# Six changes against the last waits of TensorE: row fetch, fifth output buffer, zero products, earlier first loads, halved last tile and a branch without SyncE stores in a 4096 matrix product with GELU

## The chip, the cores and the metric

The kernel runs on one core of a Trainium2 chip. The metric is the device time of one launch in microseconds, the median of the fast runs. A profiled run also has a span, from the first to the last instruction; it is about 1.6 us shorter than the run's time.

## The reference

```python
m, k, n = 4096, 4096, 4096            # a, b: float32, normal random numbers
x = np.matmul(a, b)
return 0.5 * x * (1 + np.tanh(np.sqrt(2 / np.pi) * (x + 0.044715 * x**3)))
```

## The kernel before

The product is done in float16 by a seven-product (Strassen-like) scheme over the four quadrants of `a` and `b`, in 16 output blocks (`gi`, 0 to 15). Each product (`s`, 0 to 6) has four steps (`q`) of 16 matmuls of 512 columns. VectorE forms the sums of quadrant pieces, TensorE multiplies and accumulates in two chains of banks of PSUM, its result memory (X and Y), ScalarE copies PSUM out and applies GELU, SyncE stores, and GpSimd loads with a cast to float16. An A piece is loaded into one of two staging buffers and then transposed by VectorE.

```python
PRODUCTS = [("Y", "11", ("12", "22", 1)),              # chain, A operand, B operand
            ("X", ("11", "12", -1), "22"),
            ("X", ("12", "22", -1), ("21", "22", 1)),  # third product: needs A22 and B21
            ("X", ("11", "22", -1), ("11", "22", -1)), # fourth product
            ... ]
```

For the first block the data are not there yet. Its first half of the inner dimension is done by 16 plain steps (numbers 0 to 15) as pieces arrive, and only the second half by the seven products (steps 16 on, two for each product).

A numerical check of the inputs ends in a flag. Its six statistics go through DRAM to become one row; if the flag is 0, a slow general path runs in a branch at the end.

```python
    def verdict(d):                     # called in the last block, at product 2
        for f in (0, 3):
            ...
            nc.sync.dma_start(out=row[f], in_=d...)      # fetch: behind the stores in SyncE's queue
        v = ...                          # 24 small VectorE instructions on the row
    def new_y():
        return pool.tile([P, NC], F32, name="y", tag="y", bufs=4)
    for n, step in enumerate(steps):
        for fn, args in before.get(n, ()): fn(*args)
        make_sums(...)                   # VectorE, two steps ahead of TensorE
        flush()                          # finish waiting output tiles: addition, GELU, store
        combine()
        plain(n) or multiply(*step)
with tc.If(stands == 0):
    general_path(tc, a, b, out)          # its stores: SyncE
```

## Time and profile before

| | |
|---|---|
| median | 1592.03 us at first, 1592.19 over all runs of the comparison |
| span of the profiled run | 1589.5 us |
| TensorE busy | 1570.7 us, 99% |
| lost to waits in the first 140 us, with the half clock after one of them | 9.2 us |
| lost at the verdict, with the half clock after it | 5.3 us |
| after the last product | 7.1 us |

Busy time of 99% leaves little, so the timeline of TensorE has to be read against its own grid: a group of 32 products takes 6.906 us from start to start, and each group that starts later than that has lost the difference. Half clock means a stretch in which the trace's clock records grant TensorE half of its clock. A DMA lands when the last of its sixteen shares is reported (those of the kernel's last store between 1586.06 and 1586.97). The lines are shown in the prediction.

### The profile page before, as it was taken

How to read it: one execution, taken by the hardware profiler on the slowest of the kernel's cores; microseconds unless marked ns; L12 is line 12 of the kernel's file. 1: busy time of each engine (PE TensorE's matmuls, PEld its weight loads, DVE VectorE, ACT ScalarE, POOL GpSimd, SP SyncE). 2: the span in 40 equal slices, each digit the busy share in tenths (PEclk: the TensorE clock that was granted, in tenths of full speed). 3: DMA queues.
4: the chain of work that ended last, by engine and by line, in shares of the span. 5: the costliest groups of instructions: out<-in, count | busy, mean ns of one | idle time of the engine just before them, and what ended most of it. 6: DMA issues, size and time to landing. Idle time of an engine off the chain costs nothing. (4 is left out here: it accounts for less than half of the span.)

```text
span 1589.5 us, 19678 instructions
## 1 busy us (share of the span) xinstructions
PE 1570.7 (99%) x7244; PEld 710.1 (45%) x7244; DVE 1229.0 (77%) x1370; ACT 520.9 (33%) x714; POOL 539.1 (34%) x980
## 2 busy tenths in 40 slices
PE   9999999999999999999999999999999999999998
PEld 3444444444444444444444444444444444444443
DVE  1498888967887888895878778887687778988675
ACT  0026454311122545531111344551212145454111
POOL 7663442430334144341124423245021443414300
PEclk9999999999999999999999999999999999999999
DMA  9998793891957488586597937679387886837702
GB/s 173 188 225 176 111 187 70 153 176 38 200 99 153 93 132 159 107 172 120 95 159 111 187 73 147 130 132 180 60 137 128 133 159 107 170 81 136 151 21 81
DMA packets 225048, 211.14 MB, mean 133 GB/s; under 512 B 20144, under 2 KB 192176, under 8 KB 224944
## 3 DMA queue, kind: packets, MB, share of 16 engines
q0 software_dynamic: 187648, 142.67, 61.1%
q1 hardware_dynamic: 37296, 67.13, 11.7%
q8 instruction: 59, 0.97, 0.2%
q14 instruction: 45, 0.37, 0.1%
HBM read 285.22 MB, written 67.11 MB: 222 GB/s over the span
## 5 line engine op out<-in xcount | busy, mean ns | idle before, releaser
L303 PEld LDWEIGHTS <-aS 128*128 128x128 f16 x4960 | 485.8, 98 | 590.7 <-issue 4.2
L173 POOL DMA_DIRECT2D bR<-in_b_dram x832 | 448.9, 544 | 705.5 <-DVE bS L276 335.1
L276 DVE TENSOR_TENSOR aS<-aT 128x2048 f16<-128x2048 f16 x310 | 376.5, 1221 | 154.0 <-PE accX L303 120.4
L303 PE MATMUL accX<-bS,aS 128*128 128x512 f16 x1984 | 432.8, 380 | 3.9 <-DVE bS L276 3.4
L276 DVE TENSOR_TENSOR bS<-bR 128x2048 f16<-128x2048 f16 x310 | 376.8, 1220 | 72.8 <-PE accX L303 62.1
L303 PEld LDWEIGHTS <-aT 128*128 128x128 f16 x1984 | 194.2, 98 | 236.0 <-issue 2.1
L391 ACT ACTIVATE y<-y 128x512 f32<-128x512 f32 x192 | 118.8, 631 | 338.9 <-DVE y L400 338.9
L303 PE MATMUL accY<-bS,aT 128*128 128x512 f16 x992 | 216.9, 379 | 1.8 <-DVE bS L276 1.8
L303 PE MATMUL accX<-bS,aT 128*128 128x512 f16 x992 | 216.7, 379 | 0.0
L303 PE MATMUL accY<-bS,aS 128*128 128x512 f16 x992 | 216.7, 379 | 0.0
L303 PE MATMUL accX<-bR,aS 128*128 128x512 f16 x992 | 216.7, 379 | 0.0
L303 PE MATMUL accY<-bR,aS 128*128 128x512 f16 x992 | 216.7, 379 | 0.0
L146 POOL DMA_DIRECT2D stage<-in_a_dram x144 | 90.0, 631 | 247.4 <-DVE aT L159 180.4
L400 DVE TENSOR_TENSOR energy<-energy,square 128x1024 bf16<-128x1024 bf16 x240 | 165.0, 688 | 9.2 <-ACT square L197 5.4
L197 ACT ACTIVATE square<-aT 128x1024 bf16<-128x1024 f16 x120 | 123.5, 1052 | 70.7 <-DVE energy L400 70.4
L364 ACT COPY x<-accX 128x512 f32<-128x512 f32 x128 | 74.8, 587 | 218.2 <-PE accX L303 218.2
L197 ACT ACTIVATE square<-bR 128x1024 bf16<-128x1024 f16 x120 | 123.1, 1052 | 62.4 <-DVE energy L400 62.3
L159 DVE STREAM_TRANSPOSE aT<-stage 128x2048 uint32<-128x2048 uint32 (+1 forms) x36 | 74.2, 2068 | 43.7 <-DMA stage<-in_a_dram 43.6
L364 ACT COPY m<-accX 128x512 f32<-128x512 f32 x64 | 37.2, 581 | 214.9 <-PE accX L303 214.2
L391 ACT ACTIVATE y<-accX 128x512 f32<-128x512 f32 x64 | 38.3, 598 | 101.4 <-PE accX L303 101.4
L400 DVE TENSOR_TENSOR x<-accX,x 128x512 f32<-128x512 f32 x64 | 43.9, 691 | 22.6 <-ACT y L391 21.6
L400 DVE TENSOR_TENSOR y<-accY,m 128x512 f32<-128x512 f32 x64 | 42.6, 688 | 13.5 <-ACT m L364 13.3
(37 smaller groups left out, 338.9 us busy)
## 6 DMA issues: line engine op xcount, KB each, us to landing
bR<-in_b_dram POOLq DMA_DIRECT2D x832, 128.0 KB, 5.3
out_dram<-y SPq DMA_DIRECT2D x256, 256.0 KB, 6.0
stage<-in_a_dram POOLq DMA_DIRECT2D x112, 256.0 KB, 6.9
stage<-in_a_dram POOLq DMA_DIRECT2D x32, 128.0 KB, 5.0
row<-seen_d SPq DMA_DIRECT2D x2, 1.5 KB, 2.2
seen_d<-seen SPq DMA_DIRECT2D x1, 3.0 KB, 7.5
```

The costliest lines, as they stand in the source:

```text
L146: nc.gpsimd.dma_start(out=s[g * Q : (g + 1) * Q, x : x + n, :], in_=a_v[kh * CH + c, g, :, x0 : x0 + n, :],)
L159: nc.vector.transpose(dst[:, :, x, :], src[:, :, x, :])
L173: nc.gpsimd.dma_start(out=t[g * Q : (g + 1) * Q, e::2, :], in_=b_v[kh * CH + c, g, e, :, :, n0 : n0 + NC],)
L197: nc.scalar.activation(t[:, :], src, ACT.Square)
L276: nc.vector.tensor_tensor(out=t[:, :], in0=part(tiles, blk, o[0], q), in1=part(tiles, blk, o[1], q), op=ALU.add if o[2] > 0 else ALU.subtract,
L303: nc.tensor.matmul(acc[:, :], sa[:, j // 2, i * P : (i + 1) * P, j % 2], sb[:, j, :], start=start and j == 0, stop=stop and j == 3, skip_g ...
L364: nc.scalar.copy(out=t[:, :], in_=src[:, :])
L391: nc.scalar.activation(y[:, :], src[:, :], ACT.Gelu_apprx_tanh)
L400: nc.vector.tensor_tensor(out=o[:, :], in0=x[:, :], in1=y[:, :], op=op)
```

## The change

The intent is to remove the remaining waits of TensorE and to shorten both ends. It has six parts: the row is fetched right after the statistics are written; a fifth output buffer; ten products with zero weights fill a known wait, so that the array's clock is not lowered (it was 0.5 for 3.41 us after that wait of 2.62 us); one transpose is moved a step earlier and the first A piece is loaded whole; the last tile is finished by column halves; the general path stores through GpSimd, so that the branch has no SyncE stores to wait for (SyncE's stores report on eight semaphores, called lanes here).

```diff
-    def verdict(d):
-        row = {}                                   # fetch of the row: moved to the end of gather()
+        return row
+    def verdict(row):
@@ halves of the last tile (products() takes a column slice n)
+    def last(gi, i, sa, sb):
+        y, m1 = new_y(), post.pop(("x7", i))
+        for h in range(2):
+            n = slice(h * NC // 2, (h + 1) * NC // 2)
+            products(banks["Y", i], sa, sb, i, False, True, n)
+            if h == 0:
+                flush()
+            nc.vector.tensor_tensor(out=y[:, n], in0=banks["Y", i][:, n], in1=m1[:, n], op=ALU.add)
+            emit(gi, i, 1, 1, y, y, n)
@@ fifth buffer
-        return pool.tile([P, NC], F32, name="y", tag="y", bufs=4)
+        return pool.tile([P, NC], F32, name="y", tag="y", bufs=5)
@@ zero products
+    def idle(n):
+        for _ in range(n):
+            nc.tensor.matmul(banks["X", 0][:, :], post["none"][:, :], b_tiles[0, "12", 0][:, 0, :],
+                             start=False, stop=False, skip_group_check=True)
+    before[4].append((idle, (N_IDLE,)))            # N_IDLE = 10
@@ order of the first loads
-        (8, "T21_0 B12_1 B22_1 A11_1"),
+        (7, "T21_0"),
+        (8, "B12_1 B22_1 A11_1"),
-            for h in (0, 1) if what[4] == "0" else (None,):
+            for h in (0, 1) if what[4] == "0" and what != "A11_0" else (None,):
@@ general path
-                nc.sync.dma_start(out=out[t * P : (t + 1) * P, bass.ds(n0, NC)], in_=y[:, :])
+                nc.gpsimd.dma_start(out=out[t * P : (t + 1) * P, bass.ds(n0, NC)], in_=y[:, :])
... (cuts: signatures and the zeroed weights)
```

## The prediction

Passages of the text below that no trace or run of this case shows are cut, and the cuts are marked. The forecast came to 4.42 + 2.30 + 2.17 + 1.35 - 0.1 + 0.85 = 11.0 us. One term has lost its ground: the -0.1 of the halves is their gain of 0.06 less an allowance of 0.2 us at the last store, and that allowance is cut. Without it the sum would be 11.2 us.

> **What bounds the kernel now.** I read the page's first line, then the waits of TensorE, then its timeline, then the two places where that timeline has holes, and last the records after the final matmul. The page and TensorE's list of waits:
>
> ```profile
> span 1589.5 us, 19678 instructions
> ...
> PE 1570.7 (99%) x7244; PEld 710.1 (45%) x7244; DVE 1229.0 (77%) x1370; ACT 520.9 (33%) x714; POOL 539.1 (34%) x980
> ```
>
> ```profile
> PE accX L303 <- DVE bS L276: 3.4, 1, 3.4
> PE accY L332 <- DMA bR<-in_b_dram: 2.6, 1, 2.6
> PE accY L332 <- DVE aT L159: 2.0, 1, 2.0
> PE accY L303 <- DVE bS L276: 1.8, 1, 1.8
> PE accX L315 <- DVE table L531: 1.3, 1, 1.3
> PE accX L303 <- DVE aS L276: 0.5, 1, 0.5
> ```
>
> TensorE is the bound: 7200 real products that the change does not touch. Everything to be won lies in six waits, in what follows them, and in the ends of the span. The timeline of TensorE alone tells more than the waits:
>
> ```profile
> 13.72 7.07 PE L332 MATMUL accY<-bR,aT 128*128 128x512 f16 x32
> 20.62 7.07 PE L332 MATMUL accX<-bR,aT 128*128 128x512 f16 x32
> 30.31 8.75 PE L332 MATMUL accY<-bR,aT 128*128 128x512 f16 x32 [2.62 <-DMA bR<-in_b_dram]
> 38.90 7.07 PE L332 MATMUL accX<-bR,aT 128*128 128x512 f16 x32
> 47.98 27.80 PE L332 MATMUL accY<-bR,aT 128*128 128x512 f16 x128 [2.01 <-DVE aT L159]
> ...
> 97.00 7.07 PE L303 MATMUL accX<-bS,aS 128*128 128x512 f16 x32 [0.51 <-DVE aS L276]
> ...
> 133.47 7.07 PE L303 MATMUL accY<-bS,aT 128*128 128x512 f16 x32 [1.77 <-DVE bS L276]
> ```
>
> Thirty-two products take 6.906 us from start to start (13.72 to 20.62), 0.2158 us each. Against that grid the stretch from 20.62 should have handed over at 27.53 and did so at 30.31: 2.78 us lost. The stretch from 30.31 took 8.59 us to the next start instead of 6.91: another 1.68 us, because the products ran at half speed. The wait at 47.98 cost 2.17 us and no clock. Those at 97.00 and 133.47 cost 0.66 and 1.93. After that there is no hole until the verdict, near the end:
>
> ```profile
> 1507.89 7.07 PE L303 MATMUL accX<-bS,aS 128*128 128x512 f16 x32
> ...
> 1510.73 1.22 SPq L234 DMA_DIRECT2D row<-seen_d  x2
> ...
> 1512.91 0.31 DVE L240 TENSOR_REDUCE v<-row 1x1 f32<-1x128 f32 x1 [2.44 <-DMA row<-seen_d]
> 1513.52 1.23 DVE L240 TENSOR_REDUCE v<-row 1x1 f32<-1x128 f32 x5 [0.30 <-DMA row<-seen_d]
> ...
> 1518.39 11.78 PE L303 MATMUL accX<-bS,aS 128*128 128x512 f16 x46 [3.43 <-DVE bS L276]
> ```
>
> VectorE stands 2.74 us (2.44 + 0.30) before the verdict's reductions, because SyncE fetched the row only after the last stores ahead of it in its queue; the sums that TensorE needs come behind them. TensorE should have gone on at 1514.80 and did at 1518.39 (3.59 lost). The 96 products to the next group boundary, at 1540.79, took 22.40 us instead of 20.72: 1.68 us of half clock again.
>
> [...] the clock fell after waits of 2.6 and 3.4 us and held after 2.0, 1.8 and 0.5. [...] the row fetch, moved next to the write of the scratch, will hold SyncE's queue for that write's 7.5 us (the page's table of DMA issues). [...] the stores at the end land 2.0 us after issue at the least and 3.6 at most here.
>
> **The change part by part.**
>
> Row fetch ahead. The scratch is written at 1484.40 and lands at 1491.9; the two row fetches follow (0.6 us of issue, 2.2 us to land each), so the row is there near 1495, 15 us before VectorE wants it. The one store held behind them (issued at 1484.83 now) starts near 1493; with the next output tile written near 1507 nobody wants its buffer. VectorE's 2.74 us of waiting go. Its sums end 2.74 us earlier, and TensorE's loss goes from 3.59 to 0.85 us: the 24 small verdict instructions (about 3 us) still stand before the sums. 0.85 us is under every wait that left the clock alone, so the 1.68 goes too. Gain 2.74 + 1.68 = 4.42 us.
>
> Ten zero products. They sit before the step that starts at 30.31. At 0.216 us they take 2.16 us from 27.53, to 29.69. The B piece waited for landed at 30.17. The first A piece in four DMAs of 256 KB instead of eight of 128 KB costs GpSimd some 2.5 us instead of 4.7 (0.64 against 0.58 us an issue), and in the first nine microseconds the DMA engines moved 100 to 185 GB/s against some 200 later, which is worth 1 to 1.9 us of earlier landing; so I take the piece to be there by 29.69. The step then starts at 29.69 (0.62 earlier) at full clock (1.68). Gain 2.30 us; if the landing does not move, 1.8. The first real product stays at 13.72: the 44 warm-up products end there.
>
> Transpose one step earlier. At 43.49 VectorE runs four additions (to 46.77) that no product waits for, then the transpose that TensorE waits for. The pieces for its two halves landed at 40.70 and 43.42. Moved ahead of the additions, the halves end near 41.9 and 44.7; TensorE, by now 2.3 us early, wants them at 43.5 and 47.0. No wait is left. Gain 2.17 us.
>
> Fifth output buffer. At 127.45 VectorE waits 3.18 us for the store of an earlier tile; the four tiles follow four landings (127.33, 128.74, 130.06, 131.47), and the sum that TensorE wants starts behind the last at 132.20. With five buffers the first tile finds a free one and the rest wait for the first three landings: the last ends near 130.87 and the sum starts 1.33 us earlier. Gain 1.35 of the 1.93.
>
> Last tile by halves. The last products end at 1582.4 either way. ScalarE's activation of the tile before ends at 1582.98; two half activations follow. From 512 columns at 0.587 us and 1024 at 1.052 a half is about 0.40, so ScalarE ends at 1583.78 instead of 1583.84. It has become the bound and the halves gain 0.06. The last store lands at 1586.97, its slowest sixteenth 0.6 us behind the others: [...] Net loss 0.1.
>
> Branch without store lanes. After the last landing (1586.97) SyncE passes five more lane waits (to 1587.33), then twelve waits of a second list (to 1588.12), 0.07 us each. The instruction order of the changed kernel shows the first list gone and SyncE waiting in the second, where the last store's lane is followed by only four or five. 1.2 us become about 0.35. Gain 0.85.
>
> Sum: 4.42 + 2.30 + 2.17 + 1.35 - 0.1 + 0.85 = 11.0 us. 1592.03 - 11.0 = 1581.0.
>
> **The rivals.** First, a gain at the start that is given back: from 60 to 100 us VectorE and the DMA queue are the tight chain. If the second A piece still lands at 65.45, VectorE's work from there (transposes 2.31, sums 1.2 each, the additions) reaches the four copies before the step at 97.00 only 3.8 us earlier while TensorE wants 4.47: some 0.7 us come back as a longer wait there. For it: the DMA engines are 90% busy or more to 60 us. Against it: VectorE waits for TensorE 3.7 + 0.4 us in that stretch, so it can follow. This makes 1581.7. Second, the verdict may get no cheaper if the row is late or another wait holds VectorE: the page's 7.5 us says it is not; otherwise 1585.4. Third, the zero products might be too few: if the clock falls all the same or the B piece comes later, 1583. Fourth, a gain that no wait shows, such as stores that overtake loads: I see none; TensorE's floor of 7200 x 0.2158 = 1553.8 us, plus 13.72 at the start and 7.1 at the end, is a span of 1574.6, only 4 us below the 1578.5 of my sum.
>
> **Range and chances.** The parts are independent and each is uncertain by half a microsecond to one. I take 1578.9 to 1584.3. Two per cent would be 32 us, three times all that is there to be won, so faster by that much is all but excluded; slower would need a new wait of 43 us.
>
> **What would show it.** TensorE's waits should be a list with no entry above 1.5 us; the step now at 30.31 should start near 29.7 with 32 products in 7.07 us; no wait for the transpose; the wait at 97.00 still there, 0.5 to 1.3 us, some 4.4 us earlier on the clock; the one at 133.47 about 0.6; the verdict's about 0.85, with no half-speed weight loads after it; VectorE's wait for the row gone. From the last store's landing to the end of the span there should be some 1.6 us, not 2.5. I would be wrong if a halved clock shows up after a wait under 2 us, or if the early stretch gives back more than a microsecond.

## More of the kernel before

The quadrant pieces are called by quadrant and half of the inner dimension: B21/1 is the second half of B's lower left quadrant.

The loads are issued from GpSimd's queue, in this order (in the trace of the kernel before A22/1 waits 6.21 us for its staging buffer and goes out at 68.18, and B21/1 follows it at 70.72):

```python
for n, whats in (                       # step number: A/B load a piece, T transposes an A piece
    (0, "A11_0 B12_0 T11_0 B11_0 A12_0 B22_0 B21_0 A21_0"),
    (4, "T12_0 A22_0"),
    (8, "T21_0 B12_1 B22_1 A11_1"),
    (10, "T22_0 A12_1"),
    (14, "T11_1 A22_1 B21_1 B11_1"),    # A22_1 waits for a staging buffer that T11_1 frees
    ...
```

Runs of one kernel spread by 2 us and more, and the 95% intervals of the ratios are about 0.13% (2 us) to either side. Parts worth less than that are therefore judged from stretches of the traces, not from medians.

## The result, and the profile after

The changed kernel takes 1583.76 us (median of 6, 1583.09 to 1585.01) against 1592.19 us for the kernel before in the same rounds (6 runs, 1591.26 to 1593.13). The ratio is 0.9948, interval 0.9935 to 0.9961. Ratios here are the mean time of one kernel's fast runs over that of the other's of the same rounds, so not quite the ratio of the medians. The gain of 8.4 us lies inside the predicted range, but it is 2.6 us short of the predicted 11.0.

The waits of TensorE in the changed kernel (total, times, longest, in us):

```profile
PE accX L304 <- DVE aS L277: 1.8, 1, 1.8
PE accX L304 <- ACT m L390: 1.6, 1, 1.6
PE accX L304 <- DVE bS L277: 1.5, 2, 0.9
PE accX L319 <- DVE zeros L311: 1.4, 1, 1.4
PE accY L304 <- DVE y L385: 0.7, 1, 0.7
```

The 2.6, 2.0 and 3.4 us of before are gone, but 1.8, 1.6, 0.9 and 0.7 us stand there that did not exist. TensorE's timeline tells where:

```profile
13.62 7.07 PE L344 MATMUL accY<-bR,aT 128*128 128x512 f16 x32
...
27.43 2.32 PE L326 MATMUL accX<-bR,none 128*128 128x512 f16 x10
29.59 7.07 PE L344 MATMUL accY<-bR,aT 128*128 128x512 f16 x32
...
43.41 27.79 PE L344 MATMUL accY<-bR,aT 128*128 128x512 f16 x128
...
86.02 1.90 PE L304 MATMUL accX<-bS,aS 128*128 128x512 f16 x8 [0.93 <-DVE bS L277]
89.56 5.34 PE L304 MATMUL accX<-bS,aS 128*128 128x512 f16 x24 [1.64 <-ACT m L390]
96.69 7.07 PE L304 MATMUL accX<-bS,aS 128*128 128x512 f16 x32 [1.79 <-DVE aS L277]
```

The start goes as planned. The zero products run at 27.43, the next step starts at 29.59 at full clock, and the step that stood at 47.98 starts at 43.41: 4.57 us ahead. The first block's fourth product, at 97.00 before, starts at 96.69. Of the lead 0.31 us is left; three waits in a row, at 86.02, 89.56 and 96.69, took the rest. VectorE's timeline has the reason:

```profile
80.68 1.23 DVE L277 TENSOR_TENSOR aS<-aT 128x2048 f16<-128x2048 f16 x1
84.74 1.23 DVE L277 TENSOR_TENSOR bS<-bR 128x2048 f16<-128x2048 f16 x1 [2.83 <-DMA bR<-in_b_dram]
85.88 1.22 DVE L277 TENSOR_TENSOR aS<-aT 128x2048 f16<-128x2048 f16 x1
...
88.15 2.68 DVE L426 TENSOR_TENSOR y<-accY,m 128x512 f32<-128x512 f32 x4
```

The sum for the third product waits 2.83 us for a B load. The load's records say that it is B21/1, whose last DMA landed at 84.20. In the kernel before the same piece landed at 82.40, and the same sum started at 84.52, since VectorE was busy with other work until then:

```profile
83.38 1.23 DVE L276 TENSOR_TENSOR aS<-aT 128x2048 f16<-128x2048 f16 x1
84.52 1.22 DVE L276 TENSOR_TENSOR bS<-bR 128x2048 f16<-128x2048 f16 x1
```

The load was in time by 2.1 us, unseen.

The verdict goes as predicted:

```profile
1489.00 1.22 SPq L231 DMA_DIRECT2D row<-seen_d  x2
...
1505.65 7.07 PE L304 MATMUL accX<-bS,aS 128*128 128x512 f16 x32
...
1508.14 1.48 DVE L241 TENSOR_REDUCE v<-row 1x1 f32<-1x128 f32 x6
...
1513.25 17.00 PE L304 MATMUL accX<-bS,aS 128*128 128x512 f16 x78 [0.53 <-DVE bS L277]
```

The row's fetch goes out at 1489.00, when the write of the scratch (1482.16) has landed, 6.8 us after its issue, where 7.5 were written; SyncE waited 6.5 us for it. So the row is asked for 19 us before its use, the six reductions run without a wait, and TensorE loses 0.69 us (1512.56 on the grid, 1513.25 in fact) with no half clock after it: the next group, 96 products on, starts at 1533.97, 20.72 us later.

The end, first before and then after (VectorE's addition and ScalarE's activation of the last tile; TensorE's last four products):

```profile
1582.49 0.69 DVE L400 TENSOR_TENSOR y<-accY,x 128x512 f32<-128x512 f32 x1 [0.17 <-PEq L552]
1583.21 0.63 ACT L391 ACTIVATE y<-y 128x512 f32<-128x512 f32 x1 [0.23 <-DVE y L400]
```

```profile
1575.41 0.41 DVE L385 TENSOR_TENSOR y<-accY,x 128x256 f32<-128x256 f32 x1
...
1575.88 0.60 PE L304 MATMUL accY<-bS,aS 128*128 128x256 f16 x4 [0.73 <-DVE y L385]
...
1576.51 0.42 DVE L385 TENSOR_TENSOR y<-accY,x 128x256 f32<-128x256 f32 x1 [0.69 <-PE accY L304]
1576.97 0.42 ACT L417 ACTIVATE y<-y 128x256 f32<-128x256 f32 x1 [0.51 <-DVE y L385]
```

TensorE's second half now waits 0.73 us until VectorE has read the first half. Both lie in the same PSUM tile, which is the likely reason; a version with two tiles was not run. So the work that should overlap runs in turn.

The two profiled runs differ by 7.57 us of span. It can be split at the starts of product groups, and the last landing (the fourth product itself takes 6.91 us in both and is left out):

| stretch | before, us | after, us | won |
|---|---|---|---|
| start to the first block's fourth product | 97.00 | 96.69 | 0.31 |
| first block's fifth product to second block's second (fifth buffer) | 36.46 | 34.53 | 1.93 |
| from there to the last block's second product | 1353.70 | 1353.70 | 0.00 |
| from there to its fifth product (verdict) | 46.71 | 42.13 | 4.58 |
| from there to the last store's landing (halves) | 46.17 | 46.76 | -0.59 |
| last landing to the end (branch) | 2.50 | 1.18 | 1.32 |

### The profile page after: what moved, and what is told of

The parts are those of the page before. It is cut to its first block, busy times and chain, and to the rows that moved or that the text cites. A ratio compares the mean times of both kernels' runs of the same rounds, so it can differ in the third digit from the quotient of the medians.

```text
span 1581.9 us, 19694 instructions
## 1 busy us (share of the span) xinstructions
PE 1569.4 (99%) x7258; PEld 710.7 (45%) x7258; DVE 1228.2 (78%) x1372; ACT 520.0 (33%) x715; POOL 535.5 (34%) x976
## 4 chain that ended last, share of the span: by engine, by line
PE 93%; DMA 2%; POOL 2%; DVE 1%; issue 1%; ACT 0%; DVEq 0%; ACTq 0%; POOLq 0%
PE accX L304 53%; PE accY L304 40%; DMA stage<-in_a_dram 2%; POOL stage L147 1%; POOL bR L174 1%; DMA bR<-in_b_dram 1%; DVE bS L277 0%; DVE y L426 0%; DVE aS L277 0%; DVE aT L160 0%; DVE v L241 0%; ACT m L390 0%; ACT y L417 0%; DVE y L385 0%; DVE ok L251 0%
## 5 line engine op out<-in xcount | busy, mean ns | idle before, releaser
L417 ACT ACTIVATE y<-y 128x512 f32<-128x512 f32 (+1 forms) x193 | 118.7, 627 | 337.5 <-DVE y L426 336.6
L304 PE MATMUL accY<-bS,aS 128*128 128x512 f16 (+1 forms) x996 | 216.9, 378 | 0.7 <-DVE y L385 0.7
```

Source lines behind the costliest of these rows:

```text
L304: nc.tensor.matmul(acc[:, n], sa[:, j // 2, i * P : (i + 1) * P, j % 2], sb[:, j, n], start=start and j == 0, stop=stop and j == 3, skip_g ...
L417: nc.scalar.activation(y[:, n], src[:, n], ACT.Gelu_apprx_tanh)
```

## The experiments

The theory that the trace suggests: the lead of 4.5 us at the start is real, but it runs into the arrival of B21/1, so the early parts win next to nothing (feed theory). The rival is that of the prediction: each part keeps its gain, and what is missing was lost elsewhere (additive theory). Twelve kernels were run in three sets; each set was timed beside the kernel before on its own chip.

**1. Early parts undone.** The four other parts stay.

```diff
-    before[4].append((idle, (N_IDLE,)))
-        (7, "T21_0"),
-        (8, "B12_1 B22_1 A11_1"),
+        (8, "T21_0 B12_1 B22_1 A11_1"),
-            for h in (0, 1) if what[4] == "0" and what != "A11_0" else (None,):
+            for h in (0, 1) if what[4] == "0" else (None,):
```

> The changed kernel with its three early parts undone (no zero products, the transpose back in its old step, the first A piece in eight DMAs); fifth buffer, row fetch, halves and branch stay. Feed theory (the lead won before 72 us is eaten up to the step near 97 us by VectorE's wait for the second half of B's lower left piece, which the DMA queue brings no earlier than before): slower than the changed kernel by only 0.3 us (0 to 1), TensorE's step there starts at 97.0 as before. Additive theory (my prediction): slower by 4.5 us, since each early part keeps its own gain.

Measured: 1584.61 us, ratio to before 0.9947 (0.9933 to 0.9962), where the changed kernel has 0.9948. The three early parts together are not to be seen in the time, though a difference of 2 us would not be either. The profiled run has the waits of before at 30.32 and 47.98. The fourth product started at 98.70, not at 97.0, for a reason not foreseen: after the wait before 47.98 the clock fell as well, though it had held in the kernel before after a wait of the same length. The line of TensorE's timeline:

```profile
47.98 29.49 PE L344 MATMUL accY<-bR,aT 128*128 128x512 f16 x128 [2.01 <-DVE aT L160]
```

The 128 products took 29.49 us here and 27.80 there.

**2. Early parts alone,** added to the kernel before (the same lines with the signs turned, and the zero products).

> The kernel before with the three early parts alone. Feed theory: faster than before by 0.3 us (0 to 1), the step now at 43.4 us, the one at 97.0 no earlier than 96.5. Additive theory: faster by 4.5 us.

Measured: 1592.34 us against 1592.22, ratio 1.0002 (0.9987 to 1.0017). As the feed theory has it: the step at 43.52, the fourth product at 96.35. In this trace even the 0.66 us won by then were lost again near 133 us, where the four output buffers made TensorE wait 2.7 us:

```profile
133.77 7.07 PE L304 MATMUL accY<-bS,aT 128*128 128x512 f16 x32 [2.73 <-DVE bS L277]
140.68 13.98 PE L304 MATMUL accX<-bR,aS 128*128 128x512 f16 x64
```

The clock held after this wait (6.91 us to the next start), though it was longer than the 2.01 us after which it fell in late_only; the last section comes back to this. The additive theory, with 4.5 us, falls.

**3. The same work without the wait for B21/1;** wrong (relative error 0.11), only to see the time.

```diff
+            if tag == "bS" and (mb, nb, s) == (0, 0, 2):
+                o = ("22", "22", 1)                 # B22 twice instead of B21 + B22
```

> The changed kernel, wrong on purpose: the sum that waits 2.83 us for B's lower left piece takes the piece that is already there twice, so it costs VectorE the same and waits for no load. Feed theory: the whole chain after it moves up by 2.8 us, TensorE's step at 96.69 starts near 93.9, and the run is 2.8 us faster than the changed kernel; some 2 us of hole remain before that step because VectorE began late (the second A piece landed at 66.3). If VectorE's own work is what holds the step and the load is incidental: under 1 us faster.

Measured: 1579.25 us, ratio 0.9918 (0.9904 to 0.9932), 4.5 us faster than the changed kernel's median and 4.3 faster than no_idle below, which ran beside it. The timeline of TensorE:

```profile
78.15 7.07 PE L306 MATMUL accX<-bR,aS 128*128 128x512 f16 x32
85.05 7.07 PE L306 MATMUL accX<-bS,aS 128*128 128x512 f16 x32
92.63 7.07 PE L306 MATMUL accX<-bS,aS 128*128 128x512 f16 x32 [0.51 <-DVE aS L279]
```

All three waits are gone but for the 0.5 us that the kernel before had too, and the fourth product starts at 92.63: 4.37 us earlier than before, which is the whole lead. The size was more than expected. I had left 2 us to a late start of VectorE; it did not start late in this run. By the 12.51 us of the table below, waiting for the landing at 82.42 would have put the product at 94.93, so 2.3 us of the lead are the wait's in this trace and the rest is the earlier start. The gain of the early parts was there to be had, and the wait for one load took it.

**4. No zero products.**

```diff
-    before[4].append((idle, (N_IDLE,)))
```

> The changed kernel without the ten zero products. The B piece now lands at 29.2, so TensorE waits 1.75 us instead of 2.62. If a wait of that length leaves the clock alone (2.0 us did before): the step starts at 29.3 in 32 products of 7.07 us and the total is the same within 0.3 us. If the clock falls: the step takes 8.75 us, the transposed piece's step starts 1.4 us later than 43.4, and by the feed theory the total is still the same within 0.5 us; by the additive theory 1.4 us slower.

Measured: 1583.59 us, ratio 0.9940 (0.9926 to 0.9955): the same. The step after the wait, in TensorE's timeline:

```profile
29.43 7.07 PE L344 MATMUL accY<-bR,aT 128*128 128x512 f16 x32 [1.94 <-DMA bR<-in_b_dram]
```

The wait was 1.94 us and the clock held: the B piece had landed about a microsecond earlier than in the kernel before (29.29 against 30.17). The zero products are an insurance here, not a gain. It may have counted once: in the trace of the run called best the piece landed at 31.46, and behind the zero products TensorE waited only 1.16 us and kept its clock; without them the wait would have been about 3.3 us by that trace (28.12 to 31.60, less the end of the last product), longer than the 2.62 us after which the clock fell in the kernel before.

**5 to 8. The late parts, each undone alone.**

```diff
# whole_tile: the last tile whole
-            if (gi, s, q, i) == (len(groups) - 1, NP - 1, QPH - 1, RT - 1):
-                last(gi, i, sa, sb)
-                break
# branch_sp: the general path's stores on SyncE again
-                nc.gpsimd.dma_start(out=out[t * P : (t + 1) * P, bass.ds(n0, NC)], in_=y[:, :])
+                nc.sync.dma_start(out=out[t * P : (t + 1) * P, bass.ds(n0, NC)], in_=y[:, :])
# late_row: the row fetch back at the head of verdict()
-        return row
-    def verdict(row):
+        return d                                    # gather() ends here
+    def verdict(d):
+        row = {}                                    # and the fetch follows
# four_y
-        return pool.tile([P, NC], F32, name="y", tag="y", bufs=5)
+        return pool.tile([P, NC], F32, name="y", tag="y", bufs=4)
```

> The changed kernel with the last row tile whole again. Read from the changed kernel's trace: the second half's products wait 0.73 us for VectorE to read the first half out of the same bank, so the last activation ends 0.37 us later than in the kernel before on the same grid and the last store lands 0.57 us later. If so, undoing the halves is 0.5 us faster (0.3 to 0.8) and from the last group's start to the end of the span takes 47.4 us instead of 47.9. My prediction's term (halves cost 0.1): 0.1 us faster.

Measured: 1582.73 us, ratio 0.9933 (0.9920 to 0.9946). The interval overlaps the changed kernel's (0.9948), so the timing does not resolve it. From the fifth product of the last block to the end it takes 46.07 + 1.26 = 47.33 us, against 46.76 + 1.18 = 47.94: 0.6 us faster, as the trace had said. Over all traces with the changed branch this stretch takes 47.67 to 48.03 us with halves (nine traces) and 47.32 and 47.35 without (two). The halves are a loss of 0.3 to 0.7 us.

> The changed kernel with the fallback's stores on SyncE again, so that SyncE has to wait for its eight store lanes before it leaves the branch. From the two traces: 1.70 us from the last landing to SyncE's arrival at the barrier instead of 0.38, so 1.3 us slower than the changed kernel. My prediction's term: 0.85 us slower.

Measured: 1584.51 us, ratio 0.9944 (0.9932 to 0.9956). The timing does not resolve it. In the trace the end of the span lies 2.39 us behind the last landing instead of 1.18: 1.2 us, the expected size.

> The changed kernel with the verdict row fetched late again, behind the last stores. Prediction and trace agree here: TensorE waits 3.4 us again before the verdict's sums and runs the next 3.4 to 3.8 us at half clock; 4.6 us slower than the changed kernel (4.0 to 5.0). If the gain at the verdict came from the fifth buffer or from other timing: under 2 us slower.

Measured: 1587.39 us, ratio 0.9966 (0.9953 to 0.9979), 2.9 us slower than the changed kernel by the ratios (3.6 by the medians, which come from two chips): below the expected 4.0 to 5.0, though the noise of some 3 us covers both. The verdict's stretch in the trace:

```profile
1513.64 23.61 PE L304 MATMUL accX<-bS,aS 128*128 128x512 f16 x96 [3.44 <-DVE bS L277]
1537.08 13.98 PE L304 MATMUL accX<-bS,aT 128*128 128x512 f16 x64
```

It takes 47.77 us instead of 42.13 (1489.31 to 1537.08), 5.6 us more: the wait is 3.44 us again, and the 96 products after it take 23.44 us, a longer half clock than the 22.40 of the kernel before (6.83 us in the clock records, against 3.41). The spans of the two profiled runs differ by 3.1 us only, because this one had the better start (the fourth product at 94.17 instead of 96.69); see the table below.

> The changed kernel with four output buffers. VectorE waits some 3 us again for the store near 127 us, and TensorE about 1.9 us near 133: 1.9 us slower by the traces (1.2 to 2.7), 1.35 by my prediction's term. If the shifted start already moves the stores out of the way: no difference.

Measured: 1585.57 us, ratio 0.9953 (0.9940 to 0.9965). The stretch of the fifth buffer takes 37.12 us in its trace, where the traces with five buffers and the other late parts as in the changed kernel have 34.5 to 35.7. So the buffer is worth 1.4 to 2.6 us by the traces; the ratios give 0.8, and their intervals overlap, so the timing does not resolve it.

**What sets the fourth product.** The experiments so far give the changed start several times over. B21/1 does not land at the same time in each run, and the fourth product follows it:

| trace | B21/1's last landing, us | fourth product, us | difference |
|---|---|---|---|
| whole_tile | 81.70 | 94.21 | 12.51 |
| late_row | 81.66 | 94.17 | 12.51 |
| four_y | 82.79 | 95.31 | 12.51 |
| no_idle | 82.83 | 95.34 | 12.51 |
| branch_sp | 83.72 | 96.23 | 12.51 |
| early_only | 83.83 | 96.35 | 12.51 |
| the changed kernel | 84.20 | 96.69 | 12.50 |
| the kernel before | 82.40 | 97.00 | 14.60 |
| no_b21 (does not wait for it) | 82.42 | 92.63 | 10.21 |

The constant 12.5 us is the work in VectorE's queue between: the sum itself, the sums and additions of the two steps after it, and the copy that TensorE waits for. In the kernel before there are 2.1 us more: its sum began 2.12 us after the landing instead of some 0.54, and VectorE waited 0.44 us for TensorE behind it. So the changed start keeps 0.3 to 2.8 us of its early lead from trace to trace, and the first profile happened to show nearly the worst case. Some of what is kept is lost again near 130 us: with five buffers TensorE still waited there for 0.43 us in branch_sp, 0.69 in the run called again (below), 1.02 in no_idle and 1.04 in whole_tile.

**9 to 12. The changed kernel again, and three attempts at more.**

> The changed kernel itself once more, to stand beside the three others on the same chip. In the seven traces with the early parts and the wait for B's lower left piece, the step after it (at 96.69 us in the first trace) starts 12.5 us after that piece's last landing (81.66 to 84.20 us). Feed theory: 12.5 us again, whatever the landing is. If VectorE's own work sets the step, its start does not follow the landing.

Measured: 1583.73 us, ratio 0.9955 (0.9942 to 0.9969). Landing at 82.04, fourth product at 94.56: 12.51 us once more.

```diff
# b21_early: ask for B21/1 before A22/1
-        (10, "T22_0 A12_1"),
-        (14, "T11_1 A22_1 B21_1 B11_1"),
+        (10, "T22_0 A12_1 B21_1"),
+        (14, "T11_1 A22_1 B11_1"),
# late_flush: the first block's tiles finished two steps later
-            flush()
+            if step[:2] != (0, 2):
+                flush()
# best: late_flush and whole_tile together
```

> The changed kernel with B's lower left piece asked for before A's (second) lower right piece instead of behind it, so that GpSimd's queue does not hold it back for seven microseconds until a staging buffer is free. Queue-order theory: the B piece lands near 77 us, the wait is gone and 2 to 4 us are won as in the run with the piece taken twice. Bandwidth theory: both pieces are needed for the same step and the DMA engines are full, so the A piece takes the place of the B piece, lands near 82 to 83 us and needs a transpose (2.3 us) besides: the step starts 1 to 3 us later than in the changed kernel.

Measured: 1585.21 us, ratio 0.9960 (0.9946 to 0.9974). B21/1 landed at 75.06, but A22/1 landed at 80.41 instead of 76.59 in the run beside it, and now its transpose waits (VectorE's timeline):

```profile
80.53 2.31 DVE L160 STREAM_TRANSPOSE aT<-stage 128x2048 uint32<-128x2048 uint32 x1 [3.91 <-DMA stage<-in_a_dram]
```

The fourth product starts at 95.98, 1.4 us later than in the run beside it; the time itself does not tell the two apart. The order decides which piece comes last: B21/1 came 7 us earlier and A22/1 3.8 us later. The two pieces are wanted for the same product, so the exchange wins nothing, and the one that is last now needs a transpose as well. The pair was complete at 80.41 instead of 82.04. That the loads as a whole are the limit fits this, and fits that the loads land one after another here (a 256 KB DMA every 1.3 us, with one gap of 2.2 us at A22/1 in the run beside it; in the changed kernel's first trace at 67.67, 68.95, 70.34 and 71.67, then 73.87, with the 16 DMA engines moving 160 to 202 GB/s from 60 to 84 us); a faster feed was not tried.

> The changed kernel, in which the first block's four output tiles are finished (addition, activation, store) two steps later, behind the copies that the step at 96.69 us waits for 1.79 us. The step should then start 10.7 us after the landing of B's lower left piece instead of 12.5: 1.8 us faster than the changed kernel (1.0 to 2.0), unless the later stores hold up the fifth-buffer stretch near 130 us and give it back (then 0).

Measured: 1587.41 us, ratio 0.9985 (0.9972 to 0.9999): 3.7 us slower than the changed kernel beside it, a miss. The timeline across the engines:

```profile
97.18 2.49 DVE L426 TENSOR_TENSOR y<-y,x 128x512 f32<-128x512 f32 x4
97.95 2.39 ACT L390 COPY x<-accX 128x512 f32<-128x512 f32 x4 [9.29 <-DVE y L426]
98.58 5.76 PE L304 MATMUL accX<-bS,aS 128*128 128x512 f16 x20 [5.12 <-ACT x L390]
```

The copies that TensorE waits for do not stand behind the first block's tiles only in ScalarE's order, as I had thought. They wait for those additions themselves: the copies go into the four buffers (one tag, four deep) from which the additions read. Finishing the tiles later holds the copies, and the copies hold TensorE, 5.12 us now and at half clock after it.

> The two improvements together, last tile whole and late finish of the first block's tiles: 0.6 + 1.8 = 2.4 us faster than the changed kernel, if they add.

Measured: 1587.82 us, ratio 0.9982 (0.9969 to 0.9996). It carries the same loss; its whole last tile shows again in the trace (46.12 + 1.24 us from the last block's fifth product to the end). The best version by the traces is the changed kernel with the last tile whole (1582.73 us); that it beats the changed kernel is shown in the last stretch of the traces, not in the time.

## Why the prediction was right or wrong

The total was inside the range, but the largest term, the start, failed, and that by the prediction's own sign of being wrong: "if the early stretch gives back more than a microsecond". It gave back 4.2 us in the first profile. The list of waits has entries above 1.5 us, and the wait at 97.00 did not move 4.4 us forward but stands at 96.69 with 1.79 us. "The parts are independent" was wrong too: the early parts shared one load that bounded them all. That the total held is in part luck: in the profile three other terms came out 1.2 us better in sum (and the halves 0.5 worse), and the gain of 8.4 us stayed 0.7 above the least that the range allowed.

- *Row fetch, 4.42 us.* Right: 4.58 us. TensorE loses 0.69 us where 0.85 were written, the clock holds, and undoing this part alone brings wait and half clock back.
- *Zero products, 2.30 us, and the transpose, 2.17 us.* The times were right up to 72 us: 29.59 and 43.41 against 29.69 and 43.5. But the 2.30 us are not due to the zero products: no_idle started the same step at 29.43 at full clock without them. Wrong from there on: 0.31 us of the 4.47 was left in the first profile, and 0.3 to 2.8 in the other traces with this start and this wait. The step that failed is the first rival. It reckoned with the A pieces ("If the second A piece still lands at 65.45") and with VectorE's waits for TensorE ("so it can follow"), and sized the loss at 0.7 us. It never looked at when the other operand of the third product lands. B21/1 landed at 82.40, and its sum began at 84.52: no more than 2.1 us could be kept there with that landing, whatever came before. That number was in the trace of the kernel before. A sum that did not wait for a load had been taken for a sum that would not.
- *1 to 1.9 us of earlier landing.* The B piece landed at 29.18 instead of 30.17, so 1.0 us; it had gone by the time the first A piece of the second half landed (66.32 instead of 65.45). That four DMAs instead of eight brought it is not shown: after the first sixteen B loads the lead was only 0.27 us (21.12 against 21.39), and with four DMAs the piece landed anywhere from 29.15 to 30.00 (31.46 in best). Over all traces with this start the landing of B21/1 moves between 81.66 and 84.20 (84.80 in the run called best). Most of the movement is there earlier: in the thirteen traces with this order of loads, B21/1 lands 16.8 to 17.9 us after A11/1, the first A piece of the second half, which itself moves between 64.42 and 67.99. What moves A11/1 is open, and so is the rest of 1.1 us. The one thing that stands out in the first trace is a 16 KB instruction fetch of 0.9 us at 80.7 us, with one of the sixteen shares of the loads in flight landing up to 1.3 us after the other fifteen (82.78 against 81.45). That the fetch made the lag was only seen side by side, and whole_tile, with its fetch at 79.4, landed early all the same.
- *Fifth buffer, 1.35 us.* A little low: 1.93 us in the profile, 1.4 to 2.6 across traces. In the profile the first of the waited-for stores landed 3.72 us after issue instead of 5.26.
- *Halves, -0.1 us.* The sign was right, though it came from the allowance of 0.2 us; the size was 0.6. The term knew only ScalarE and the stores; the wait of TensorE between the halves, 0.73 us, was not in it. A halved product took 0.108 to 0.109 us from start to start.
- *Branch, 0.85 us.* Low: 1.32 us in the profile and 1.21 by the run that undoes it. The passing of SyncE's lane waits was right; 0.37 us between its last two steps, which I had left standing, also went.
- *Clock.* "A halved clock after a wait under 2 us" was named as what would prove me wrong; none was seen. At 2.0 us it went either way; the first point of the last section has what sorts the cases in these traces.

## What to carry to other kernels

When a wait is removed in a stretch fed by loads, list for every later operand of that stretch when it lands and when it is first used, not only the operands that somebody waits for today: the smallest slack in that list is the most that can be kept, as long as the landings stay where they are. Here the start won 4.5 us and lost 1.7 to 4.2 of them 40 us later, to a load that had been in time by 2.1 us. And splitting a tile to overlap two engines won nothing here, where both halves lay in one tile and one engine waited for the other between them.

## What the traces show of the half clock, the instruction fetches and the end of the branch

- Half clock. In the clock records of the fourteen traces each stretch of half clock between the warm-up and the last product lasts 3.41 or 6.83 us, and those of one trace lie on one grid of 3.41 us (in the kernel before the two begin at 30.74 and 1518.95, 436 steps of 3.413 us apart). Laid over TensorE's waits, this grid sorts every case of these traces: the clock fell where 2.01 us or more of one such window were idle (2.01, 2.07, 2.17, 2.62, 2.82, 2.86, 2.88, 3.41), and held where no window had more than 1.94. The length of the wait alone does not sort them: 2.01 us fell in late_only, in one window, and held in the kernel before, cut into 1.84 and 0.17; the 2.43 us of four_y (0.64 and 1.79) and the 2.73 us of early_only (1.90 and 0.83) held. This was worked out from the traces afterwards, and no run was made to test it. The 1.94 us of no_idle stand at the very edge.
- Instruction fetches. At the end of the kernel before, instruction fetches of 16 KB at 1583.19 us and 8 KB at 1583.94 ran beside the last stores, and one sixteenth of the last store landed 0.6 us after the other fifteen, at 1586.97. The link is read from the times and not tested; the records do not say on which DMA engine a fetch ran.
- Leaving the branch. It took 2.4 to 2.5 us from the last landing to the end with pending store lanes (2.50 in the kernel before, 2.39 in branch_sp), and 1.2 to 1.3 without (1.18 in the changed kernel).
